# Re-cut loads, a second load ahead of the opening barrier, and a first store timed by its copies, in an im2col kernel

## Chip, cores, metric

One core of a Trainium2 chip. The metric is the device time of one execution in microseconds; medians are of the runs named. The profile's span starts with the first instruction and is about 1.78 us shorter than the time (e3 below is an exception).

## The reference

The kernel unfolds 3x3 patches of an image batch (im2col). Nothing is computed: 4.19 MB are read and 33.18 MB are written.

```python
# x: (16, 64, 32, 32) float32, kernel_size 3
for b in range(batch):
    col_idx = 0
    for i in range(h_out):           # 30
        for j in range(w_out):       # 30
            patch = x[b, :, i:i + kernel_size, j:j + kernel_size].copy()
            cols[b, :, col_idx] = patch.ravel()
            col_idx += 1
return cols                          # (16, 576, 900) float32
```

## The kernel before

Each of 128 partitions holds eight channels of one image (`CPP = 8`, 32 KB). A channel becomes nine shifted copies of 30x30 (32,400 bytes) in an output tile; channels 0 and 1 are stored one by one, the others in pairs from two alternating tiles. ScalarE and VectorE share the copies two to three, and the sync engine (SP) issues all transfers on one queue. `H` is 32. At the opening barrier all engines wait for one another before the kernel's own work; it passes at 0.7 us in the trace.

```python
cuts = [0, H, 200, CPP * H]                  # rows of 128 bytes: loads of 4, 21 and 7 KB per partition
first = load(nc.sync, cuts[0], cuts[1])      # later moved ahead of the opening barrier
bulk = load(nc.sync, cuts[1], cuts[2])
load(nc.sync, cuts[2], cuts[3])

on_act = (False, True, False, True, False)
n = 0
for c in range(0, CPP, 2):
    out_tile = out_pool.tile([P, 2, KK, HO, WO], x.dtype, name="out_tile")   # two buffers
    for s in range(2):
        for kk in range(KK):
            ...
            if on_act[n % len(on_act)]:
                nc.scalar.copy(out=dst, in_=src)
            else:
                nc.vector.tensor_copy(out=dst, in_=src)
            n += 1
        if c == 0:
            st = nc.sync.dma_start(out=out_v[:, s], in_=...)
            if s == 0:
                tc.add_manual_dep(st.ins, bulk.ins.name, ...,
                                  reason="the store follows the bulk of the loads")
    if c > 0:
        nc.sync.dma_start(out=out_v[:, c : c + 2]..., in_=...)
# ... after compiling: the first load is moved ahead of SP's drain, that is, of the opening barrier
```

## Time and profile before

| | before |
|---|---|
| time, 3 runs at first | 91.44, 91.50 and 92.87 us (the last, 1.6% above the fastest, counts as slow) |
| time of the profiled run | 91.84 us |
| profiled span | 90.1 us |
| DMA packets' share of 16 engines | 97.0% |
| ScalarE, VectorE busy | 29%, 26% |
| loads end, mean and last of 16 DMA engines | 11.68, 12.21 us |
| stores end, mean and last | 88.31, 88.77 us |

The lower rows come from the trace's packet records: each of the 16 DMA engines works through its own packets one after the other. The records do not number the engines; a packet is given to the engine whose last packet ended where it starts. The time is set by the engine that ends last.

### The profile page before, as it was taken

How to read it: one execution, taken by the hardware profiler on the slowest of the kernel's cores; microseconds unless marked ns; L12 is line 12 of the kernel's file. 1: busy time of each engine (PE TensorE's matmuls, PEld its weight loads, DVE VectorE, ACT ScalarE, POOL GpSimd, SP SyncE). 2: the span in 40 equal slices, each digit the busy share in tenths (PEclk: the TensorE clock that was granted, in tenths of full speed). 3: DMA queues.
4: the chain of work that ended last, by engine and by line, in shares of the span. 5: the costliest groups of instructions: out<-in, count | busy, mean ns of one | idle time of the engine just before them, and what ended most of it. 6: DMA issues, size and time to landing. Idle time of an engine off the chain costs nothing.

```text
span 90.1 us, 140 instructions
## 1 busy us (share of the span) xinstructions
DVE 23.5 (26%) x43; ACT 26.2 (29%) x30; POOL 0.2 (0%) x4
## 2 busy tenths in 40 slices
DVE  0380399970000089600000399300000000000000
ACT  5391399940000089920000399300000000000000
POOL 0000000000000000000000000000000000000000
DMA  5999899999599999993799999999999999947990
GB/s 129 486 382 449 360 518 446 460 460 446 259 460 460 691 460 432 460 432 173 345 460 460 460 460 460 460 460 460 460 460 460 460 432 460 403 201 345 460 460 0
DMA packets 1152, 37.37 MB, mean 415 GB/s; under 512 B 128, under 2 KB 128, under 8 KB 384
## 3 DMA queue, kind: packets, MB, share of 16 engines
q1 hardware_dynamic: 1152, 37.37, 97.0%
HBM read 4.19 MB, written 33.18 MB: 415 GB/s over the span
## 4 chain that ended last, share of the span: by engine, by line
DMA 45%; DVE 16%; DVEq 1%; issue 0%; SPq 0%
DMA out_dram<-out_tile 35%; DVE out_tile L57 16%; DMA in_tile<-in_x_dram 11%; DVEq L93 1%; DVEq L57 0%; SPq L75 0%
## 5 line engine op out<-in xcount | busy, mean ns | idle before, releaser
L55 ACT COPY out_tile<-in_tile 128x900 f32<-128x900 f32 x29 | 24.9, 938 | 30.1 <-DMA out_dram<-out_tile 25.3
L57 DVE COPY out_tile<-in_tile 128x900 f32<-128x900 f32 x43 | 23.5, 624 | 33.6 <-DMA out_dram<-out_tile 26.0
L55 ACT ACT_TABLE_LOAD x1 | 1.3, 1283 | 0.8 <-PEq L122 0.8
L122 POOL MEMSET const-bfloat16-1.0<- 128x1 bf16 x1 | 0.1, 102 | 0.0
L122 POOL MEMSET const-uint8-127<- 128x1 uint8 x1 | 0.1, 102 | 0.0
L122 POOL MEMSET const-float32-0.0<- 128x1 f32 x1 | 0.1, 99 | 0.2 <-issue 0.2
L122 POOL MEMSET const-float32-1.0<- 128x1 f32 x1 | 0.1, 99 | 0.0
## 6 DMA issues: line engine op xcount, KB each, us to landing
out_dram<-out_tile SPq DMA_DIRECT2D x3, 8100.0 KB, 31.3
out_dram<-out_tile SPq DMA_DIRECT2D x2, 4050.0 KB, 14.9
in_tile<-in_x_dram SPq DMA_DIRECT2D x1, 2688.0 KB, 9.6
in_tile<-in_x_dram SPq DMA_DIRECT2D x1, 896.0 KB, 11.4
in_tile<-in_x_dram SPq DMA_DIRECT2D x1, 512.0 KB, 3.6
```

The costliest lines, as they stand in the source:

```text
L55: nc.scalar.copy(out=dst, in_=src)
L57: nc.vector.tensor_copy(out=dst, in_=src)
L93: tc.compile()
L122: nc = _bacc.Bacc("TRN2", target_bir_lowering=False, num_devices=1)
```

## The change

Its intent: start the input sooner (two loads ahead of the barrier, 1 and 11 KB per partition, then 20 KB), and drop the dependency of the first store. Instead channel 0's copies, five on ScalarE and four on VectorE, are to end at the right moment.

```diff
-    cuts = [0, H, 200, CPP * H]
-    first = load(nc.sync, cuts[0], cuts[1])
-    bulk = load(nc.sync, cuts[1], cuts[2])
+    cuts = [0, 8, 3 * H, CPP * H]
+    first = [load(nc.sync, r0, r1) for r0, r1 in zip(cuts[:2], cuts[1:3])]
     load(nc.sync, cuts[2], cuts[3])
...
-                if on_act[n % len(on_act)]:
+                if kk % 2 == 0 if c + s == 0 else on_act[n % len(on_act)]:
...
-                st = nc.sync.dma_start(
+                nc.sync.dma_start(
                     out=out_v[:, s], ...
-                if s == 0:
-                    tc.add_manual_dep(st.ins, bulk.ins.name, ...)
...
-    load = first.ins                     # one load moved ahead of SP's drain
+    for load in (f.ins for f in first):  # both are
```

More of the change, by code (lines that the diff above doesn't have):

```diff
@@ L63, in _im2col @@
                 )
-                if s == 0:
-                    tc.add_manual_dep(
-                        st.ins,
-                        bulk.ins.name,
-                        mybir.DependencyInfo(
-                            mybir.DependencyClass.Sync, mybir.DependencyReason.DATA
-                        ),
-                        reason="the store follows the bulk of the loads",
-                    )
         if c > 0:
@@ L94 @@
     blocks = tc.nc.main_func.blocks
-    load = first.ins
-    home = next(b for b in blocks if any(i.name == load.name for i in b.instructions))
-    home.instructions = [i for i in home.instructions if i.name != load.name]
-    head = list(blocks[0].instructions)
-    at = next(
-        k
-        for k, i in enumerate(head)
-        if i.engine == load.engine and type(i).__name__ == "InstDrain"
-    )
-    head.insert(at, load)
-    blocks[0].instructions = head
+    for load in (f.ins for f in first):
+        home = next(
+            b for b in blocks if any(i.name == load.name for i in b.instructions)
+        )
+        home.instructions = [i for i in home.instructions if i.name != load.name]
+        head = list(blocks[0].instructions)
+        at = next(
+            k
+            for k, i in enumerate(head)
+            if i.engine == load.engine and type(i).__name__ == "InstDrain"
+        )
+        head.insert(at, load)
+        blocks[0].instructions = head
 _INS = ['x', 'kernel_size']
```

## The prediction

> **What bounds the kernel now.** I read the page's busy shares first, then its DMA rows, then the queue's share, then the order of instructions in time.
>
> ```profile
> DVE 23.5 (26%) x43; ACT 26.2 (29%) x30; POOL 0.2 (0%) x4
> ...
> DMA  5999899999599999993799999999999999947990
> ...
> q1 hardware_dynamic: 1152, 37.37, 97.0%
> HBM read 4.19 MB, written 33.18 MB: 415 GB/s over the span
> ```
>
> Both copying engines are idle for 70% of the span, while the packets of the one DMA queue fill 97.0% of sixteen engines' time. The dips in the 40-slice row (a 3 and a 7 near 41 us, a 4 and a 7 near 80 us) look like holes but are not: a slice is 2.25 us and a 64,800-byte packet is counted where it starts. I took the packet records of the trace and spread each packet over its own duration (median 2394 ns for 64,800 bytes, 1200 ns for 32,400, 799 ns for 21,504, 272 ns for 7168, 159 ns for 4096). So read, all sixteen engines are busy from about 1.5 us to 88.0 us, at 405 to 430 GB/s while the loads run and 432 to 433 GB/s while the stores run. Per engine that is a first packet at 1.0 to 1.35 us, 10.6 us of loads (1.77 + 6.64 + 2.18), 76.7 us of stores (19.24 + 57.51) and an end near 88.3 us. One engine ends at 88.77 us: it fell 0.5 us behind in the second load and never caught up. Landing and closing barrier take 1.3 us more, to 90.1. So the kernel is at its transfer bound, and **only three things can move its end**: when the first packet starts, how slow the loads are, and any time in which an engine has an empty queue.
>
> The place to look is the joint between loads and stores:
>
> ```profile
> 0.00 1.60 SPq L35 DMA_DIRECT2D in_tile<-in_x_dram  x3
> ...
> 0.79 1.28 ACT L55 ACT_TABLE_LOAD   x1 [0.79 <-PEq L122]
> 3.61 3.48 ACT L55 COPY out_tile<-in_tile 128x900 f32<-128x900 f32 x4 [1.54 <-DMA in_tile<-in_x_dram]
> 3.61 2.78 DVE L57 COPY out_tile<-in_tile 128x900 f32<-128x900 f32 x5 [3.61 <-DMA in_tile<-in_x_dram]
> 10.43 8.54 ACT L55 COPY out_tile<-in_tile 128x900 f32<-128x900 f32 x10 [3.35 <-DMA in_tile<-in_x_dram]
> ...
> 10.50 3.67 SPq L60 DMA_DIRECT2D out_dram<-out_tile  x2
> ```
>
> The columns are start, duration, engine, line and operation, and in brackets the idle time before and what ended it. Channel 0 is copied by 7.1 us, but its store is issued only at 10.50 us, when the bulk load has landed. By the packet records each engine ends its loads at 11.53 to 11.75 us (the slow one at 12.21), mean 11.65, and the first store packet follows at 11.54 us without a gap. The store is in the queue about 1 us before it is needed: no slack is wasted and none is missing. Note also the table load of ScalarE: it runs at 0.79 us, under the first load, and costs nothing.
>
> **What the Trainium skill says.**
> - "DMA: Bandwidth & Descriptors", section "Where 436 GB/s comes from": 435 GB/s is the ceiling of the SBUF ports. The 433 GB/s of the stores agrees, so no rate is left to win. The same section expects some 358 GB/s between HBM and SBUF; this trace differs, and the trace decides.
> - The same page, "Queues, rings and completion order": an engine takes its ring's descriptors in order. The trace agrees: the first store packets start only where an engine's loads are over. So a store issued early cannot delay loads issued before it, and the removed dependency buys or costs nothing by itself.
> - "ScalarE: Activation LUTs", "What ACT_TABLE_LOAD costs": 1283 ns for the table load, about 1380 ns for a drain beside it, 186 ns + 0.833 ns per element for an ACTIVATE, and 93 ns of overlap back to back. The trace has 1283 ns for the table load and 938 ns for a 900-element copy (the rule gives 936), with starts 845 ns apart. Whether a drain follows is hidden before by a 1.54 us wait.
>
> **The change, part by part.**
>
> *Loads.* The same 4.19 MB in packets of 1024, 11,264 and 20,480 bytes. From the medians above, a packet costs about 8.4 ns + 0.0368 ns per byte: 46, 422 and 761 ns. Eight of each per engine make 9.83 us, against 8 x (159 + 799 + 272) = 9.84 us before. No difference. The start-up cost of the first packets (about 0.5 us per engine in the first load: 1.77 less 1.27) should stay. Two issues ahead of the barrier put the barrier some 0.4 us later (one issue takes 0.38 us), and the third load is issued near 1.2 us, long before its turn. Queue dry in the loads: no. Mean end of loads per engine again 11.65 us.
>
> *First channel.* All nine copies of channel 0 now need the second load (rows 8 to 96), whereas before they needed only the first. An engine reaches its end at 1.56 us (first packet plus start-up) + 8 x (46 + 422) ns = 5.3 us, plus 0.1 us for slow packets; the last engine some 0.4 us later (as in the first load before, 3.22 against a mean of 2.83). A semaphore is seen 0.38 us after the last packet (3.22 to 3.61, 10.06 to 10.43). So the second load is known at about **6.1 us** (5.8 to 6.5).
>
> *A displaced table load.* The order of instructions shows something that the diff does not. ScalarE's first copy now has two loads to wait for; an instruction carries one such wait, so the wait for the second load stands as an instruction of its own, and the table load comes behind it. The 1.28 us that were hidden at 0.79 us now begin when the second load has landed. VectorE has no such thing.
>
> *The first store.* ScalarE has five of the copies (4 x 0.845 + 0.938 = 4.32 us), VectorE four (3 x 0.538 + 0.63 = 2.2 us), so ScalarE decides: 6.1 + 0.05 + 1.28 + 4.32 = 11.75 us, issue 0.07 us later at **11.8 us** instead of 10.50. The first load's packet came 1.0 us after its issue; for a store into an empty queue I take 0.6 to 1.0 us, so first packets near 12.6 us, mean over engines 12.7 us. The queue's loads end at 11.65: **a hole of about 1.05 us on an average engine**, which was nil.
>
> *After that.* Channel 1: ScalarE has three more, done at 14.3 us; the second store is issued near 14.4, needed only at 12.7 + 9.6 = 22.3 us. The next one follows at about 20.3 us, needed at 31.9. Later stores all stand in the queue 10 us or more early, as before. The stores' 76.7 us per engine are unchanged, so the hole is passed on to the end in full, with one rebate: the engine that was 0.5 us late with its loads was the one that set the end; in the hole it catches up, and it will be late only if the same happens in the stores. Mean end 12.7 + 76.65 = 89.35, last engine about 89.6, against 88.77: +0.8 us on the profiled run. In timed runs without so late an engine (91.44 and 91.50 against 91.84 profiled) it is up to +1.1 us. Sum: 91.5 + 1.0 = **92.5 us**.
>
> **The rivals.**
> 1. *No hole: the store comes just in time.* If the table load did not wait, the store would be issued at 6.1 + 4.32 + 0.1 = 10.5 us, the very moment of before, and the time would be 91.3 to 91.6. For it: the change says that the copies are to time the store, and 10.5 fits too well to be chance. Against it: the order of instructions. A smaller variant has a faster start with 1 KB packets, so that the second load lands 0.3 us earlier; that shifts the whole chain, for 92.2.
> 2. *A drain behind the table load.* If the 1.38 us of the skill's page come on top, the store is issued at 13.2 us and the hole is 2.4 us: 93.8 us, slower by 2.5%. For it: the page. Against it: copies are a filler function, there is no earlier table work to drain, and no drain of that kind stands in the trace of before.
> 3. *Loads get faster or slower.* If the late engine comes from the 21,504-byte load's first packet (one took 1381 ns), new sizes may spare it or repeat it. Either way it is worth at most 0.5 us, and the hole hides most of that. This goes into the range.
>
> **Range and chances.** My own sum gives 92.2 to 93.0 with the landing of the second load and the issue latency as its doubts. Rival 1 (some 15%) pulls the low end down, rival 2 (some 8%) would lie above the range. Range 91.6 to 93.1. Two per cent slower is 93.3, which needs rival 2 or all doubts on one side: 0.1. Two per cent faster (89.7) would need 1.8 us out of a transfer that has no hole to close: 0.01.
>
> **What would show it.** Right: the table load starts at 6 us and not at 1; ScalarE's first copy 1.3 us behind VectorE's first; the first store is issued near 11.8 us and ends ScalarE's, not VectorE's, copies; the packet records show engines idle around 12 us for about 1 us; stores again at 433 GB/s; later stores all issued before they are needed. Wrong: a first store at 10.5 us with no hole (rival 1), a gap between table load and first copy (rival 2), loads that end well off 11.65 us, or a second hole, for instance a store of channels 2 and 3 later than 32 us.

## The result, and the profile after

The changed kernel takes **92.79 us** (median of 6 runs, 92.73 to 92.92) against 91.68 us (median of 5 fast runs, 91.44 to 92.41; the slow one of 92.87 is left aside). The ratio is 1.0114, 95% interval 1.0074 to 1.0154: slower by about one per cent. Ratios here compare the mean times of fast runs of the same rounds, so they are not quite the ratio of the medians. 92.5 us had been predicted, 91.6 to 93.1.

The page of the changed kernel, first its busy shares, then DMA share and moved bytes by slice of 2.28 us:

```profile
DVE 22.9 (25%) x42; ACT 26.9 (30%) x31; POOL 0.2 (0%) x4
...
DMA  6899959999789999999999999999994699999990
GB/s 147 371 461 432 432 228 456 456 456 441 327 370 456 456 456 456 456 456 456 456 456 456 456 456 456 456 456 456 456 427 199 285 456 456 456 456 456 456 456 0
...
q1 hardware_dynamic: 1152, 37.37, 96.1%
```

The sixth slice (11.4 to 13.7 us) is new: DMA busy falls to 5 tenths and the rate to 228 GB/s. By the packet records the engines are idle there, not slow: every 20,480-byte packet took 761 to 764 ns. The order of instructions in time says why:

```profile
6.42 1.28 ACT L55 ACT_TABLE_LOAD   x1 [6.42 <-DMA in_tile<-in_x_dram]
6.45 11.38 DVE L57 COPY out_tile<-in_tile 128x900 f32<-128x900 f32 x21 [6.45 <-DMA in_tile<-in_x_dram]
7.72 12.76 ACT L55 COPY out_tile<-in_tile 128x900 f32<-128x900 f32 x15
12.06 2.87 SPq L60 DMA_DIRECT2D out_dram<-out_tile  x2
20.50 0.33 SPq L65 DMA_DIRECT2D out_dram<-out_tile  x1
```

ScalarE loads its table when the second load has landed, 6.42 us, and not at 0.79. Its first copy stands 1.27 us behind VectorE's. The first store is issued at 12.06 us, while the loads end at 11.77 us (mean of the engines). The critical chain names the same pieces, in order of time (start, duration, what):

```profile
0.43 5.92 DMA in_tile<-in_x_dram
...
6.37 0.02 ACTq L55
...
6.42 1.28 ACT L55
...
7.72 12.77 ACT out_tile L55 x15
...
20.50 31.41 DMA out_dram<-out_tile
```

The piece at 6.37 us is an instruction of its own in ScalarE's queue that does nothing but wait for the second load; the table load stands behind it. By the packet records the first store packets start at 12.91 to 13.06 us, mean 12.97: a hole of 1.20 us on the average engine, where there was none. The store packets then take 76.8 us per engine (76.7 before); the engines end at 89.70 us on average, the last at 89.81.

### The profile page after: what moved, and what is told of

The parts are those of the page before. It is cut to its first block, busy times and chain, and to the rows that moved or that the text cites. A ratio compares the mean times of both kernels' runs of the same rounds, so it can differ in the third digit from the quotient of the medians.

```text
span 91.0 us, 140 instructions
## 1 busy us (share of the span) xinstructions
DVE 22.9 (25%) x42; ACT 26.9 (30%) x31; POOL 0.2 (0%) x4
## 3 DMA queue, kind: packets, MB, share of 16 engines
q1 hardware_dynamic: 1152, 37.37, 96.1%
## 4 chain that ended last, share of the span: by engine, by line
DMA 41%; ACT 15%; DVE 6%; DVEq 1%; SPq 0%; issue 0%; ACTq 0%
DMA out_dram<-out_tile 35%; ACT out_tile L55 14%; DMA in_tile<-in_x_dram 7%; DVE out_tile L57 6%; ACT L55 1%; DVEq L83 1%; SPq L35 0%; DVEq L57 0%; ACTq L55 0%
## 5 line engine op out<-in xcount | busy, mean ns | idle before, releaser
L55 ACT COPY out_tile<-in_tile 128x900 f32<-128x900 f32 x30 | 25.6, 938 | 24.7 <-DMA out_dram<-out_tile 24.7
L57 DVE COPY out_tile<-in_tile 128x900 f32<-128x900 f32 x42 | 22.9, 624 | 35.2 <-DMA out_dram<-out_tile 28.7
L55 ACT ACT_TABLE_LOAD x1 | 1.3, 1283 | 6.4 <-DMA in_tile<-in_x_dram 6.4
```

## The experiments

All outputs are right. "Loads end" and "hole" are means over the 16 engines, from the packet records of the profiled run. A hole is the time between an engine's last load packet and its first store packet.

### e1: take the table load's wait away

```diff
+    warm = in_pool.tile([P, 1], x.dtype, name="warm")
+    nc.scalar.copy(out=warm, in_=in_flat[:, 0:1])   # waits for the 1 KB load alone
```

> The changed kernel with a one-element copy on ScalarE that waits for the first load alone, so that the table load stands ahead of the wait for the second load. My theory (the displaced table load opens a hole in the queue): the table load runs near 1.3 us, ScalarE's first large copy starts with VectorE's at about 6.4 us, the first store is issued near 10.8 us instead of 12.06, no engine waits for it, and the time is 91.75 us (91.5 to 92.0), 1.1 us under the changed kernel; it is not the full 1.2 us of the hole because the engine that ends its loads last then sets the end again. The runs should spread more than the 0.2 us of the changed kernel. Rival A (the small first load or the two issues ahead of the barrier cost the time): still 92.7 to 92.9. Rival B (copies and loads disturb each other): between the two.

Measured: 91.88 us (91.81 to 92.0), ratio 1.0030 (1.0016 to 1.0044).

```profile
1.25 1.28 ACT L43 ACT_TABLE_LOAD   x1 [1.25 <-PEq L116]
2.54 0.19 ACT L43 COPY warm<-in_tile 128x1 f32<-128x1 f32 x1
6.53 11.08 ACT L57 COPY out_tile<-in_tile 128x900 f32<-128x900 f32 x13 [3.79 <-DMA in_tile<-in_x_dram]
6.60 10.84 DVE L59 COPY out_tile<-in_tile 128x900 f32<-128x900 f32 x20 [6.60 <-DMA in_tile<-in_x_dram]
10.87 2.88 SPq L62 DMA_DIRECT2D out_dram<-out_tile  x2
```

The loads and the split are those of the change, and most of the loss is gone (ratio 1.003 against 1.011). The store goes out 1.19 us sooner, and the hole is 0.08 us. So the place of the table load is the cause, not the small first load. The runs spread by 0.19 us, not more than those of the change: that part of the expectation missed.

### e2: one load instead of two ahead of the barrier

```diff
-    cuts = [0, 8, 3 * H, CPP * H]
-    first = [... zip(cuts[:2], cuts[1:3])]
-    load(nc.sync, cuts[2], cuts[3])
+    cuts = [0, 3 * H, CPP * H]
+    first = [... zip(cuts[:1], cuts[1:2])]
+    load(nc.sync, cuts[1], cuts[2])
```

> The changed kernel with its first two loads joined into one of 12 KB per partition, ahead of the barrier. ScalarE's first copy then has one wait only. My theory: the table load goes back to about 0.8 us without any added instruction, first store near 10.8 us, no hole, 91.7 us (91.4 to 92.0). Rival A: if the small packets at the start are what costs, it is as fast, but then the first run of this call is not; so only the two together tell. If the number of waits were not the reason for the table load's place, the table load would stay at 6.4 us and the time at 92.8.

Measured: 91.53 us (91.37 to 91.61), ratio 0.9990 (0.9975 to 1.0005).

```profile
0.78 1.28 ACT L55 ACT_TABLE_LOAD   x1 [0.78 <-PEq L114]
6.20 11.08 ACT L55 COPY out_tile<-in_tile 128x900 f32<-128x900 f32 x13 [4.14 <-DMA in_tile<-in_x_dram]
...
10.54 2.88 SPq L60 DMA_DIRECT2D out_dram<-out_tile  x2
```

With one load to wait for, the table load is early again with no instruction added. The hole is 0.01 us. This confirms that the second wait put the table load where it was. It is also 0.35 us faster than e1: its loads end 0.2 us sooner (11.57 against 11.76 us) and its store packets wait for nothing.

### e3: leave the table load late, but give ScalarE less

```diff
-                if kk % 2 == 0 if c + s == 0 else ...
+                if kk % 3 == 1 if c + s == 0 else ...   # three copies on ScalarE
```

> The changed kernel with three of channel 0's copies on ScalarE and six on VectorE; the table load stays behind the wait. My theory: ScalarE ends channel 0 at 7.72 + 2 x 0.845 + 0.94 = 10.35 us, VectorE at 6.45 + 5 x 0.538 + 0.63 = 9.8, the store is issued at 10.4 us, no hole, 91.75 us (91.5 to 92.0), although the table load is as late as before. Rival: if a late table load costs in another way (or the hole has another cause), it stays at 92.7 or more.

Measured: 92.07 us (92.05 to 92.17), ratio 1.0050 (1.0036 to 1.0065).

```profile
6.42 1.28 ACT L55 ACT_TABLE_LOAD   x1 [6.42 <-DMA in_tile<-in_x_dram]
...
10.37 3.03 SPq L60 DMA_DIRECT2D out_dram<-out_tile  x2
```

The store is issued at 10.37 us, the hole is 0.04 us and the span is 90.1 us against 91.0, as the theory says: within the span the late table load costs only the hole that it opens. The time misses the expected range by 0.07 us. In each of its five runs the time is 2.05 to 2.11 us above the span, against 1.74 to 1.84 us in the other experiments. These 0.28 us lie outside the profile; their cause is open, so that a late table load costs nothing else is not shown.

### e4: make the hole larger

```diff
-                if kk % 2 == 0 if c + s == 0 else ...
+                if kk > 0 if c + s == 0 else ...        # eight copies on ScalarE
```

> The changed kernel with eight of channel 0's copies on ScalarE and one on VectorE, three more than the five of the change: a larger hole on purpose. My theory: the first store is issued 3 x 0.845 = 2.54 us later, at 14.6 us, the hole grows from about 1.2 to 3.75 us, and all of it reaches the end: 92.8 + 2.5 = 95.3 us (95.1 to 95.5), with runs as close together as those of the changed kernel. Rival: if later slack takes up part of a hole, less than 94.5 us.

Measured: 95.26 us (95.2 to 95.36), ratio 1.0399 (1.0383 to 1.0415).

```profile
DMA  6899905999999999998759999999999999999990
GB/s 143 376 443 429 403 0 222 443 443 443 443 443 443 443 665 443 443 443 360 305 249 416 443 443 443 443 443 443 443 443 443 443 443 443 443 443 443 443 443 0
```

There is one slice in which no packet starts (the view counts a packet where it starts; the last load packets run on to 12.11 us). The store was issued at 14.62 us, 2.56 us later than in the change; the hole grew by 2.52 us (3.72 against 1.20) and the span by 2.54 (93.57 against 91.03). A hole is paid in full.

### e5: the kernel before, without the dependency

```diff
-                if s == 0:
-                    tc.add_manual_dep(st.ins, bulk.ins.name, ...)
```

> The kernel before with only the dependency of the first store on the bulk load taken away. The first store is then issued when channel 0 is copied, near 7.2 us instead of 10.5, with 4.5 us of loads still ahead of it in the queue. My theory (each engine takes its queue in order, and the kernel is at its transfer bound): the first store packets still start where the loads end, 11.5 us and later, no change: 91.55 us (91.35 to 91.8). Rival: if stores mixed in among loads slow the loads, or let the copies start later, 92 us or more; if an earlier store helps, under 91.2.

Measured: 92.84 us (median of four fast runs, 92.73 to 92.92; one slow run of 94.32 left aside), ratio 1.0127 (1.0081 to 1.0172). **My theory fell here**: I had said that this dependency buys nothing. Busy share and rate of its page, and below them the rate in the kernel before:

```profile
DMA  5999999999988999999999999999999787899990
GB/s 121 469 416 435 205 426 456 456 456 456 427 370 384 413 456 456 456 456 456 456 456 456 456 456 456 456 456 456 456 456 427 313 370 342 370 456 456 456 456 0
...
GB/s 129 486 382 449 360 518 446 460 460 446 259 460 460 691 460 432 460 432 173 345 460 460 460 460 460 460 460 460 460 460 460 460 432 460 403 201 345 460 460 0
```

In the fifth slice (9.1 to 11.4 us) DMA is at 9 tenths and yet moves 205 GB/s (360 before). That is not a hole; the engines are busy with slow packets. The timeline shows the store standing in the queue at the time:

```profile
7.09 6.73 SPq L60 DMA_DIRECT2D out_dram<-out_tile  x2
```

The 7168-byte packets of the third load took 415 ns on average; in the kernel before they took 272. The loads ended at 12.93 us instead of 11.68. The first store packet still started only where an engine's loads ended, so the order is kept; it is the loads that suffer.

### e6: the kernel before with the new split of channel 0 only

```diff
-                if on_act[n % len(on_act)]:
+                if kk % 2 == 0 if c + s == 0 else on_act[n % len(on_act)]:
```

> The kernel before with only the split of channel 0's copies changed (five on ScalarE, four on VectorE). With its first load of 4 KB, ScalarE starts at 3.6 us with its table already loaded and ends near 7.9 us, far ahead of the bulk load that the first store waits for. My theory: no change, 91.55 us (91.35 to 91.8), first store again at 10.5 us. Rival: if the split by itself cost time, 92 us or more.

Measured: 91.62 us (91.4 to 92.23), ratio 0.9999 (0.9961 to 1.0037). The first store went out at 10.31 us. The split costs nothing as long as the dependency holds the store.

### e7: the change with the old split of channel 0

```diff
-                if kk % 2 == 0 if c + s == 0 else on_act[n % len(on_act)]:
+                if on_act[n % len(on_act)]:             # four copies of channel 0 on ScalarE
```

> The changed kernel with the old split of channel 0's copies (four on ScalarE): loads and dropped dependency alone. The table load stays late, at 6.4 us; ScalarE ends 0.845 us sooner, the first store is issued at 11.2 us, its packets start at 12.05 us, a hole of 0.25 to 0.4 us. Theory: 92.1 us (91.9 to 92.3), between the joined-load version (91.5) and the change (92.8); the three-copies version without a hole stood at 92.07, of which 0.28 us lay outside the profiled span, so this one may show 92.0 to 92.2 by either count. Rival: if the hole were not what counts, the time of the change, 92.8.

Measured: 92.11 us (91.95 to 92.2), ratio 1.0043 (1.0011 to 1.0075). The store was issued at 11.38 us and the hole is 0.49 us. One copy fewer on ScalarE takes 0.7 us off the hole.

### e8: only one load ahead of the barrier

```diff
-    for load in (f.ins for f in first):
+    for load in (f.ins for f in first[:1]):
```

> The changed kernel with its second load behind the opening barrier, as the bulk load of the kernel before was: only one load ahead of it. The second issue moves from 0.43 to about 0.79 us. The 1 KB load ends per engine at 1.45 to 1.78 us in the changed kernel, and a packet follows its issue by about 0.85 to 1.0 us, so some engines stand empty for 0.1 to 0.2 us. Theory: the second load lands 0.1 to 0.2 us later and everything after it too, 92.9 us (92.75 to 93.1). If the early issue is worth nothing: 92.8; if more hangs on it: over 93.2.

Measured: 93.53 us (93.24 to 93.87), ratio 1.0185 (1.013 to 1.024). Beside the change the loss is 0.7 us by the medians, 0.5 us in the profiled runs (93.34 against 92.82), not 0.1 to 0.2. The second load's first packets (mean of the 16 earliest) started at 1.99 us against 1.67, because each engine stood empty between the two loads for 0.42 us on average instead of 0.10; its last packet ended at 6.55 against 6.02. ScalarE could start only when the slowest engine had landed, so the first store was issued at 12.59 us:

```profile
6.94 1.28 ACT L55 ACT_TABLE_LOAD   x1 [6.94 <-DMA in_tile<-in_x_dram]
...
12.59 2.88 SPq L60 DMA_DIRECT2D out_dram<-out_tile  x2
```

So the early issue of the second load is worth 0.3 us here, in its start. The other 0.2 us in the profiled run are a slower last engine, which this run alone does not tell from chance.

### e9: an attempt at something better, 8 KB first

From e2, loads of 8 and 24 KB:

```diff
-    cuts = [0, 3 * H, CPP * H]
+    cuts = [0, 2 * H, CPP * H]
```

> Attempt at a version better than both: one load of 8 KB per partition (two channels) ahead of the barrier, then one of 24 KB, no dependency, the split of the change. Table load early (one wait), first store near 9.3 us, 2 us before its turn in the queue. By my theory nothing is left to win but start-up: 91.5 us (91.2 to 91.7), the same as before within half a per cent. If an earlier store or fewer loads gave more than that, under 91.1.

Measured: 91.71 us (91.6 to 91.73), ratio 1.0002 (0.9971 to 1.0033). The store was issued at 9.15 us. The 24,576-byte packets took 912 ns, and 1003 to 1150 ns from 10 us on (means by half microsecond). The time is at the top end of the expected range, and the theory had no slow packets in it.

### e10 and e11: what is it that slows the loads?

e10 takes e5 and joins its second and third loads into one of 28 KB per partition:

```diff
-    cuts = [0, H, 200, CPP * H]
+    cuts = [0, H, CPP * H]
-    load(nc.sync, cuts[2], cuts[3])
```

> The kernel before without the dependency (which ran at 92.9 us, with its 7 KB load packets slowed from 272 to 415 ns on average) and with its second and third loads joined into one of 28 KB per partition. The first store is issued near 7.1 us again, with 3.5 us of loads still to move, now in large packets. Theory T1 (a store that stands queued within an engine's reach behind loads slows each of their packets by some 0.25 us): three or four packets of 1.06 us are hit, loads end 0.5 to 1.0 us late, 92.1 to 92.6 us. Theory T2 (the loss comes from a third load that begins when a store is already queued, or from its small packets): no slow packets, 91.5 us. Theory T3 (loads run at half rate for as long as a store is queued): over 94 us.

Measured: 92.76 us (92.64 to 93.37), ratio 1.0105 (1.0053 to 1.0156). Nearly all packets took 1062 to 1090 ns until about 9 us (means by half microsecond), then some 1700 to 1900 ns, the very last less: a loss of 600 to 800 ns each, not 250. T2 falls (no third load, no small packets), T3 falls (the store stood there from 6.92 us, the loss began at about 9), and T1's figure falls.

e11 takes e5 and cuts its first store in two:

```diff
+                for k0, k1 in ((0, 4), (4, KK)) if s == 0 else ((0, KK),):
+                    nc.sync.dma_start(out=out_v[:, s, k0 * HO * WO : k1 * HO * WO], ...)
```

> The kernel before without the dependency, its first store cut into two of 14,400 and 18,000 bytes per partition, the first of them issued near 5.3 us. The lost 1.25 us per engine were about the time of one 32,400-byte store packet (1.2 us). If one store packet is fetched ahead of the loads and its time is lost (T4), the loss shrinks to 0.5 to 0.7 us: 92.1 us. If the loss goes by load packets (T1), it stays: 92.8 us or, as the store stands there earlier, more. If it goes by the time a store is queued (T3): clearly more, 93.5 us or over.

Measured: 92.93 us (92.88 to 93.18), ratio 1.0119 (1.007 to 1.0167). T4 falls: store packets of half the size lose as much. The first store was issued at 5.36 us, 1.7 us sooner than in e5, and the loss was no larger.

What the three early stores have in common: issued at 5.36, 6.92 and 7.09 us, with load packets of 7 or 28 KB and store packets of 14 or 32 KB, the loads slowed near 9 to 9.5 us, when 54 to 71 KB per engine were left, ran at 200 to 260 GB/s from 10 to 12 us (427 GB/s from 10 to 11 us in the kernel before), and ended at 12.9 to 12.95 us in all three. The loss is about 1.2 us per engine each time. The copies are no rival cause: in e10 neither engine copies between 6.9 and 13.4 us, and its packets slow all the same.

```profile
3.41 3.48 ACT L54 COPY out_tile<-in_tile 128x900 f32<-128x900 f32 x4 [1.35 <-DMA in_tile<-in_x_dram]
3.41 2.78 DVE L56 COPY out_tile<-in_tile 128x900 f32<-128x900 f32 x5 [3.41 <-DMA in_tile<-in_x_dram]
6.92 10.26 SPq L59 DMA_DIRECT2D out_dram<-out_tile  x2
13.43 4.32 ACT L54 COPY out_tile<-in_tile 128x900 f32<-128x900 f32 x5 [6.54 <-DMA in_tile<-in_x_dram]
```

That a store standing queued behind the last loads slows them is shown (e5 alters nothing else). Why, and why just so much, is not.

### e12: a little later

From e9, six instead of five copies on ScalarE:

```diff
-                if kk % 2 == 0 if c + s == 0 else ...
+                if kk % 3 != 1 if c + s == 0 else ...
```

> The version with one 8 KB load ahead of the barrier, which issued its first store at 9.15 us and showed its last load packets slowed from 912 to some 1000 to 1150 ns from 10 us on, now with six instead of five of channel 0's copies on ScalarE, so that the store is issued 0.85 us later, at 10.0 us. From the runs so far the time lies in a valley over the moment of the first store: 92.8 us at 6.9, 91.7 at 9.15, 91.5 at 10.5, 92.1 at 11.4, 92.8 at 12.06, 95.3 at 14.6. Theory: fewer slowed packets than at 9.15 us and no hole, 91.45 us (91.2 to 91.65), level with the kernel before. If the slowed packets stay, their cause is not how long the store stands queued, and the time is 91.7.

Measured: 91.45 us (91.4 to 91.8), ratio 0.9992 (0.9976 to 1.0007).

```profile
0.80 1.28 ACT L55 ACT_TABLE_LOAD   x1 [0.80 <-PEq L114]
4.83 9.38 ACT L55 COPY out_tile<-in_tile 128x900 f32<-128x900 f32 x11 [2.75 <-DMA in_tile<-in_x_dram]
...
10.02 2.87 SPq L60 DMA_DIRECT2D out_dram<-out_tile  x2
```

Every 24,576-byte packet took 912 ns, and there is no hole. It has the lowest median of all and is level with the kernel before within the interval. No version beat that kernel by an amount that the runs can tell.

### All of them, by the moment of the first store

| kernel | first store issued, us | median, us | ratio | hole, us | loads |
|---|---|---|---|---|---|
| e11 | 5.36 | 92.93 | 1.0119 | 0 | slowed |
| e10 | 6.92 | 92.76 | 1.0105 | 0 | slowed |
| e5 | 7.09 | 92.84 | 1.0127 | 0 | slowed |
| e9 | 9.15 | 91.71 | 1.0002 | 0 | slowed at the end |
| e12 | 10.02 | 91.45 | 0.9992 | 0 | |
| e6 | 10.31 | 91.62 | 0.9999 | 0.01 | |
| e3 | 10.37 | 92.07 | 1.0050 | 0.04 | |
| before | 10.50 | 91.5 to 91.7 | 1 | 0 | |
| e2 | 10.54 | 91.53 | 0.9990 | 0.01 | |
| e1 | 10.87 | 91.88 | 1.0030 | 0.08 | |
| e7 | 11.38 | 92.11 | 1.0043 | 0.49 | |
| **the change** | 12.06 | 92.79 | 1.0114 | 1.20 | |
| e8 | 12.59 | 93.53 | 1.0185 | 1.42 | |
| e4 | 14.62 | 95.26 | 1.0399 | 3.72 | |

It is a valley. The kernels differ in their loads and splits too, so this is a trend, not a curve of one variable. To its left the queued store slows the loads, to its right the queue runs dry. Only e3 stands off it, by the 0.28 us outside its span.

## Why the prediction was right

The time and the mechanism were right. By its own steps:

- *Bound, and what can move the end.* Right, with two loose readings: the loads' mean end of 11.65 us leaves out the late engine (11.68 with it), and the rate of 405 GB/s is reached from 2.5 us on, not from 1.5. The share of the queue fell from 97.0 to 96.1%, and e4 shows that a hole is passed on in full (2.52 us of hole, 2.54 us of span).
- *The displaced table load.* Right, and it is the cause: at 6.42 us it ran 1.28 us, the next copy followed 11 ns later, and e1 and e2 take it away, each in its own way. No drain followed it, so rival 2 is out. Rival 1's time, 91.3 to 91.6 us, is what e2 shows once the table load is out of the way (91.53); e1, at 91.88, comes within 0.3 us of it.
- *When the second load is known.* 6.1 us predicted (its terms add up to 6.18), 6.37 measured. I had put 0.1 us of slow packets into this load beyond the start-up in the first one. In fact nearly all the start-up cost moved into it: its packets took 505 ns on average instead of 422 (0.66 us per engine), those of the 1 KB load 56 instead of 46. And "Queue dry in the loads: no" was off by a little: between the first load and the second each engine stood empty for 0.10 us on average, by the packet records (none before). The total excess of the loads stayed as before, 0.74 us against 0.75, so rival 3 counted for nothing in the mean.
- *The first store.* 11.8 us predicted, 12.06 measured; the 0.26 us are those of the landing. Its packets came 0.84 us after the issue (0.6 to 1.0 was taken).
- *The hole.* 1.05 us predicted, 1.20 measured. *The end:* last engine 89.6 us predicted, 89.81 measured; span 0.97 us longer where 0.8 had been summed for the profiled run.
- *The rebate for the late engine.* Consistent: the engine that ended its loads last at 12.09 us had no lag at the end of the stores, where all sixteen lay between 89.62 and 89.81 us (88.16 to 88.77 before). Which of them had been late can't be followed across the hole, and no run tests the rebate by itself.

Two side steps were wrong without touching the number. "The removed dependency buys or costs nothing by itself" fell with e5: alone it costs 1.3%. It did not show in the change, where the store is issued at 12.06 us and the loads end at 11.77. And I gave the second load's place ahead of the barrier no value; e8 says that without it the change would have lost some 0.7 us more.

## What to carry to other kernels

When an instruction gets a second thing to wait for, look in the built order at what stands between the two waits: a fixed cost that was hidden, such as ScalarE's table load, may now start only after the first of them. In this kernel, which is at its transfer bound, the moment of the first store has an optimum: late, it leaves a hole that is paid in full; early, here, it slowed the loads still in front of it, so a dependency that looks superfluous should be taken out by itself before it is dropped. Read the DMA share and the rate together: a low share with a low rate is a hole, a full share with a low rate is slow packets, and they call for opposite cures.

## What the Trainium skill lacked or had wrong

- "DMA: Bandwidth & Descriptors", section "Where 436 GB/s comes from": it lets HBM bind at about 358 GB/s between HBM and SBUF. That does not hold for the one core here: the stores ran at 432 to 433 GB/s in every trace, near its fabric ceiling of 435. Beside its table of measured rates the page itself says that 358 holds with both cores of a pair at work, so it is this sentence that needs the condition.
- The same page, "Queues, rings and completion order": the order within a ring holds in these traces, but it does not say that a store queued behind loads slows them. Here the last loads ran at 200 to 260 GB/s instead of 427, for a loss of about 1.2 us (e5, e10, e11).
- "ScalarE: Activation LUTs", "What ACT_TABLE_LOAD costs": 1283 ns agrees. The drain of about 1380 ns that it gives for a switch did not follow this first load of the program: the next copy started 11 ns after it. The page puts the load right before the instruction that needs it, but does not say that it can be caught behind a wait for data, as here at 6.42 instead of 0.79 us.
- "DMA: Bandwidth & Descriptors", "Latency and other measured facts": some 600 ns to the first byte, without saying from when. From the end of the issuing instruction to the first packet the traces show 0.50 us for a store into an empty queue and 0.62 us for the first load; from its start it is 0.84 and 1.0 us.
